# Stick-breaking heads: one summed softplus tile per key block in place of up to three products

## The chip, the cores and the metric

One NeuronCore of a Trainium2 chip runs the whole kernel as one program. The metric is the device time of one execution in microseconds (us). The engines are named as in the profile: PE is the matrix engine and PEld its weight loads, DVE the vector engine, ACT the scalar engine, POOL the general engine; SP issues most of the DMAs. Each engine works through its own list of instructions in order, and an instruction that waits holds back all that stand behind it on that engine.

## What is computed

One transformer block on 512 tokens of width 1024: 16 heads of stick-breaking attention, 4 heads of retention, two sigmoid branch gates, a gated merge and a feed-forward part, all in float32. The change touches the stick-breaking heads alone. Cut to what matters, per head:

```python
z = einsum('td,sd->ts', q, k) * scale           # queries t, keys s, in blocks of 128
mask = s_pos < t_pos
log_1m_beta = where(mask, log_sigmoid(-z), 0)   # = -softplus(z) where the mask holds
after = cumsum(log_1m_beta, reverse=True) - log_1m_beta   # sum over the later keys
a = where(mask, exp(log_sigmoid(z) + after), 0)
out = a @ v
```

For a key in block j, `after` is the sum over the later keys of its own block and over all keys of the later blocks. The cumulative sum runs over the keys, which lie on the partitions here (keys by queries), so it is made by matmuls: a triangular matrix of -1 for a block's own keys, a full matrix of -1 for each later block.

## The kernel before

Every float32 operand is split in two float32r parts: ACT copies it rounded (`hi`, L207) and DVE subtracts that from the source (`lo`, L209). A product with an exact operand (the -1 matrices) takes two matmuls, one for each part; a product of two split operands takes three.

The stick-breaking heads run in four groups of four, `sb_head(h)` for h = 0 to 15. A head has four key blocks j = 0 to 3; block j meets the queries from 128 j on, so its scores are 512, 384, 256 and 256 columns wide. `GEO` gives each block its PSUM bank: block 0 in bank 0, block 1 in bank 1, blocks 2 and 3 side by side in bank 2. The three banks `z` come from a pool of three, so a head's scores take the banks that the head before it gives free. A head is, for bank 2, 1, 0 in turn:

1. PE: the scores, k by q (`z<-q,q`), two matmuls for a block.
2. DVE: the mask by a minimum (L607), minus the absolute value by setting the sign bit (L609). ACT: exp (L612), log(1+x) (L613). DVE: max(z, 0) plus that, the softplus (L614). ACT and DVE: its split into `hi` and `lo`.
3. PE: `negtri` by the own block and `negones` by each later block, added to the scores in the bank. PE is the only engine that reads the softplus tiles.
4. ACT: exp of the bank (L630); ACT and DVE: split of it; PE: the product with v into the bank `av`. ACT copies `av` out (L642), a DMA on SP's list moves half of it to other partitions (L644), DVE adds the halves (L645).

Between the heads stand other pieces that PE can do meanwhile: `sb_qk(p)`, the q and k of a later pair of heads (48 matmuls 512 wide), whose results a DMA copies into tiles of the pool `q`, and 16 branch gates, `gate(i)` (24 matmuls 512 wide each, read by DVE in L827, then three activations). Their weights arrive by DMA and are split by ACT and DVE, 1024 columns at a time (`whi`, `wlo`). After the last head come the products with `w_proj_sb`, which need all heads.

The pool `q` has 8 buffers; a pair of heads holds three of them. The order of all instructions on each engine in this part is chosen by a scheduler when the program is built, from priorities (the program's order) and its own estimate of when operands are ready; nothing is written out by hand.

Of the kernel before, what the change touches and what calls it, by code (L numbers as in the profile page):

```python
# [19 lines left out]
P = 128  # L20
# [90 lines left out]
GEO = ((0, 0, 0, 512), (1, 0, 128, 384), (2, 0, 256, 256), (2, 256, 256, 256))  # L111
# [4 lines left out]
def kernel(  # L116
# [9 lines left out]
    nc = tc.nc  # L126
# [22 lines left out]
    def pair(tag):  # L149
        return apool.tile([P, 2, S], F32R, tag=tag, bufs=BUFS[tag], name=nm(tag))  # L150
# [44 lines left out]
    negtri = cpool.tile([P, P], F32R, name="negtri")  # L195
# [32 lines left out]
    def mm(o, lhs, rhs, start, stop):  # L228
        return nc.tensor.matmul(o, lhs, rhs, start=start, stop=stop, skip_group_check=True).ins  # L229
# [208 lines left out]
    with tc.manual_schedule(engines={nc.vector.engine, nc.scalar.engine, nc.tensor.engine}):  # L438

        nc.scalar.preload_act_table_set("natural_log_exp_and_others")  # L440
        c = sm[:, SM_C : SM_C + KT]
# [152 lines left out]
    def sb_head(h):  # L594
        q, k, vt = sbq[h], sbk[h], sbv[h // 4]
        z = [psz(), psz(), psz()]
        for j in (3, 2, 1, 0):
            bank, c, t0, w = GEO[j]
            for i in range(2):
                head_pe[h] = mm(z[bank][:, c : c + w], k[:, j * P : (j + 1) * P], q[:, i, t0:S],  # L600
                                i == 0 and j != 2, i == 1)
        sp = {}
        for bank in (2, 1, 0):
            w = BANKW[bank]
            zb = z[bank][:, :w]
            m = S if bank == 2 else P
            nc.vector.tensor_tensor(zb[:, :m], zb[:, :m], maskc[:, :m], op=ALU.min)  # L607
            t = tmp()[:, :w]
            nc.vector.tensor_scalar(  # L609
                t.bitcast(I32), zb.bitcast(I32), -(2**31), None, op0=ALU.bitwise_or  # L610
            )
            nc.scalar.activation(t, t, AF.Exp)  # L612
            nc.scalar.activation(t, t, AF.Ln, bias=1.0)  # L613
            nc.vector.scalar_tensor_tensor(t, zb, 0.0, t, op0=ALU.max, op1=ALU.add)  # L614
            hl = pair("s")
            split(hl[:, 0, :w], hl[:, 1, :w], t)
            sp[bank] = hl
        avs = {}
        for bank in (2, 1, 0):
            for j in (3, 2) if bank == 2 else (bank,):  # L620
                _, c, t0, w = GEO[j]
                terms = [(negtri, j, t0)] + [(negones, jj, GEO[jj][2]) for jj in range(j + 1, 4)]
                for lhs, jj, tt in terms:
                    bj, cj, tj, wj = GEO[jj]
                    for i in range(2):
                        mm(z[bank][:, c + tt - t0 : c + w], lhs, sp[bj][:, i, cj : cj + wj],
                           False, False)
            w = BANKW[bank]
            t = tmp()[:, :w]
            nc.scalar.activation(t, z[bank][:, :w], AF.Exp)  # L630
            hl = pair("s")
            split(hl[:, 0, :w], hl[:, 1, :w], t)
            avs[bank] = hl
        o = psa()
        r, hf = (h % 4) // 2, h % 2
        for j in (3, 2, 1, 0):
            bank, c, t0, w = GEO[j]
            v = vt[j // 2][:, j % 2, r * 256 + hf * P : r * 256 + hf * P + P]
            for i in range(2):
                mm(o[:, t0:S], v, avs[bank][:, i, c : c + w], j == 3 and i == 0, j == 0 and i == 1)  # L640
        u, u2 = tmp(), tmp()
        nc.scalar.activation(u, o, AF.Copy)  # L642
        own, oth = (slice(0, HD), slice(HD, P)) if hf == 0 else (slice(HD, P), slice(0, HD))
        nc.sync.dma_start(u2[own], u[oth])  # L644
        nc.vector.tensor_add(o_sb[h // 2][own], u[own], u2[own])  # L645
# [1082 lines left out]
```

## Time and profile before

| | |
|---|---|
| time, median of 3 runs | 1173.23 us (1172.66 to 1174.77) |
| span of the profiled execution | 1173.1 us |
| PE busy | 1156.8 us (99%), 6476 matmuls |
| DVE busy | 873.2 us (74%), 1342 instructions |
| ACT busy | 611.9 us (52%), 928 instructions |
| first mask (L607) of head 0, of head 1, of head 15 | 492.61, 502.44, 710.93 us |
| last product with v of head 15 | 726.80 us |

The page gives the profiled execution by its span, from its first to its last instruction; that is 0.1 us from the median of the runs, so spans and times can be compared as they stand. The heads take the stretch from about 490 to 727 us. A matmul's busy time contains the tail of its pipeline: what one costs in a stream is the distance from one start to the next, not its duration.

### The profile page before, as it was taken

To read this page: it belongs to the slowest core of one execution; us is meant where nothing else is said; L and a number is where in the kernel's file an instruction comes from. 1 tells how busy PE (TensorE), PEld (TensorE's weight loads), DVE (VectorE), ACT (ScalarE), POOL (GpSimd) and SP (SyncE) were. 2 spreads that over 40 slices of the span, in tenths; PEclk is the share of its full clock that TensorE was granted. 3 is DMA by queue.
4 is the path that set the end of the run, shared out by engine and by line. 5 is a ranking of instruction groups with operands and counts; after the bars stand their busy time and mean duration, and the time that the engine had idled before them with its cause. 6 is when DMAs were issued, how large, how long until landed. Compare 5 with 4: busy or idle time off the path is not lost.

```text
span 1173.1 us, 16899 instructions
## 1 busy us (share of the span) xinstructions
PE 1156.8 (99%) x6476; PEld 1010.9 (86%) x6476; DVE 873.2 (74%) x1342; ACT 611.9 (52%) x928; POOL 50.1 (4%) x84
## 2 busy tenths in 40 slices
PE   8999999999999999999999999999999999999996
PEld 7898888888878888888888888879999999999996
DVE  7979966775764867478888688775998776777556
ACT  5444543343333444478778688354954444454433
POOL 0000000020002010000000000000100000000000
PEclk9999999999999999999999999999999999999999
DMA  9723536493566565846565545873545663565232
GB/s 358 256 68 113 185 103 208 154 260 115 161 201 176 181 159 185 232 123 180 153 173 133 153 126 179 283 235 103 113 136 179 184 161 116 148 186 152 86 89 72
DMA packets 64017, 192.88 MB, mean 164 GB/s; under 512 B 7744, under 2 KB 9920, under 8 KB 63936
## 3 DMA queue, kind: packets, MB, share of 16 engines
q1 hardware_dynamic: 56624, 172.92, 46.3%
q0 software_dynamic: 6768, 18.35, 8.8%
q8 instruction: 51, 0.84, 0.3%
q10 hardware_dynamic: 544, 0.52, 0.1%
q14 instruction: 30, 0.25, 0.1%
HBM read 146.15 MB, written 18.87 MB: 141 GB/s over the span
## 4 chain that ended last, share of the span: by engine, by line
PE 89%; DVE 4%; DMA 3%; ACT 2%; issue 1%; SPq 0%; DVEq 0%; ACTq 0%
PE ps L229 65%; PE z L229 21%; PE av L229 3%; DMA raw<-wp 2%; DMA araw<-wada 1%; DVE sraw L387 1%; ACT whi L207 1%; DVE wlo L209 1%; DMA o<-xT 0%; ACT s L207 0%; DVE wlo L418 0%; DVE t L425 0%; DVE araw L257 0%; DMA gspill<-g 0%; DVE t L476 0%
## 5 line engine op out<-in xcount | busy, mean ns | idle before, releaser
L229 PE MATMUL ps<-h,whi 128*128 128x512 f32 (+1 forms) x1410 | 416.9, 377 | 1.6 <-DVE h L209 0.8
L229 PEld LDWEIGHTS ps<-h,whi 128*128 128x128 f32 x1410 | 256.2, 188 | 47.7 <-ACT h L431 1.8
L229 PE MATMUL ps<-h,wlo 128*128 128x512 f32 (+1 forms) x705 | 262.1, 376 | 0.0
L207 ACT ACTIVATE whi<-raw 128x1024 fp32r<-128x1024 f32 (+1 forms) x122 | 127.4, 1044 | 192.3 <-PE ps L229 144.8
L209 DVE TENSOR_TENSOR wlo<-raw,whi 128x1024 fp32r<-128x1024 f32 (+1 forms) x122 | 146.6, 1204 | 61.9 <-ACT whi L207 60.8
L229 PEld LDWEIGHTS ps<-h,wlo 128*128 128x128 f32 x705 | 132.8, 188 | 23.2
L229 PE MATMUL ps<-s,whi 128*128 128x512 f32 x480 | 148.5, 390 | 0.7 <-DVE v L209 0.6
L229 PE MATMUL z<-q,whi 128*128 128x256 f32 x504 | 106.8, 283 | 0.0
L229 PEld LDWEIGHTS ps<-s,whi 128*128 128x128 f32 x480 | 89.2, 188 | 19.3 <-DVE v L209 1.0
L229 PE MATMUL ps<-s,wlo 128*128 128x512 f32 x240 | 93.4, 389 | 0.0
L207 ACT ACTIVATE s<-t 128x512 fp32r<-128x512 f32 (+1 forms) x134 | 74.4, 586 | 34.8 <-DVE t L789 21.4
L209 DVE TENSOR_TENSOR s<-t,s 128x512 fp32r<-128x512 f32 (+1 forms) x134 | 81.3, 637 | 9.6 <-ACT s L207 9.3
L229 PEld LDWEIGHTS z<-q,whi 128*128 128x128 f32 x504 | 84.9, 192 | 1.5
L1166 DVE SCALAR_TENSOR_TENSOR o<-ps,mod,o 128x512 f32<-128x512 f32 (+1 forms) x63 | 42.4, 680 | 32.6 <-PE ps L229 32.6
L229 PEld LDWEIGHTS ps<-s,wlo 128*128 128x128 f32 x240 | 45.1, 188 | 9.5
L877 ACT ACTIVATE whi<-s 128x1024 fp32r<-128x1024 f32 x33 | 34.9, 1056 | 33.6 <-PE ps L229 19.0
L229 PE MATMUL ps<-whi,h 128*128 128x512 f32 (+1 forms) x192 | 52.4, 354 | 0.0
L881 DVE TENSOR_TENSOR wlo<-s,whi 128x1024 fp32r<-128x1024 f32 x32 | 39.1, 1222 | 16.3 <-ACT whi L877 15.9
L229 PE MATMUL ps<-q,whi 128*128 128x256 f32 (+1 forms) x224 | 49.3, 313 | 0.0
L229 PE MATMUL z<-qp,whi 128*128 128x256 f32 x168 | 47.2, 283 | 0.0
L229 PE MATMUL z<-q,wlo 128*128 128x256 f32 x168 | 46.4, 283 | 0.0
L257 DVE SCALAR_TENSOR_TENSOR araw<-araw,cact 128x1024 f32<-128x1024 f32 x32 | 38.4, 1221 | 10.0 <-DMA araw<-wada 9.8
(311 smaller groups left out, 2063.1 us busy)
## 6 DMA issues: line engine op xcount, KB each, us to landing
raw<-wp SPq DMA_DIRECT2D x151, 512.0 KB, 4.0
araw<-wada SPq DMA_DIRECT2D x32, 512.0 KB, 4.5
araw<-wp SPq DMA_DIRECT2D x26, 512.0 KB, 4.6
sraw<-wada SPq DMA_DIRECT2D x16, 512.0 KB, 7.8
q<-qp SPq DMA_DIRECT2D x32, 256.0 KB, 3.7
s<-wp SPq DMA_DIRECT2D x12, 512.0 KB, 5.2
spill<-o POOLq DMA_DIRECT2D x24, 256.0 KB, 7.2
o<-xT SPq DMA_DIRECT2D x16, 256.0 KB, 3.7
```

Of the source, the lines that this page charges most:

```text
L207: nc.scalar.activation(dst_hi, src, AF.Copy, scale=scale)
L209: return (eng or nc.vector).tensor_sub(dst_lo, src, f(dst_hi))
L229: return nc.tensor.matmul(o, lhs, rhs, start=start, stop=stop, skip_group_check=True).ins
L257: nc.vector.scalar_tensor_tensor(raw, raw, 1.0, cact, op0=ALU.mult, op1=ALU.mult, accum_out=col)
L387: nc.vector.scalar_tensor_tensor(raw, raw, 1.0, cact, op0=ALU.mult, op1=ALU.mult, accum_out=col)
L877: nc.scalar.activation(hi, t, AF.Copy)
L881: nc.vector.tensor_sub(lo, t, f(hi))
L1166: return nc.vector.scalar_tensor_tensor(x1[d][:, hv], o[:, hv], mod[:, gcol + d : gcol + d + 1], x1[d][:, hv], op0=ALU.mult, op1=ALU.add,)
```

## The change

`sb_head` makes two sums of softplus tiles on DVE, splits each of them as the tiles themselves are split, and gives them to `negones` in place of the tiles that they sum:

- When bank 2 is done (blocks 2 and 3), `late` = block 2 + block 3, 256 columns: one add (L620 in the new numbering), one copy on ACT, one subtraction on DVE. Block 1 multiplies `late` once, where it multiplied blocks 2 and 3.
- When bank 1 is done, `later` = block 1 + `late`, 384 columns in all (the add L625 covers 256 of them): again one add, one copy, one subtraction. Block 0 multiplies `later` once, where it multiplied blocks 1, 2 and 3.

`late` and `later` take buffers of the pool `q`. A head has 6 matmuls of 256 columns less on PE (2 for block 1, 4 for block 0), 4 instructions more on DVE and 2 more on ACT. From L628 on, line numbers of the new kernel are 13 higher than before: L630 is L643, L642 is L655, L645 is L658, L827 is L840.

```diff
--- before.py
+++ after.py
@@ -615,16 +615,29 @@
             hl = pair("s")
             split(hl[:, 0, :w], hl[:, 1, :w], t)
             sp[bank] = hl
+            if bank == 2:
+                late = pair("q")
+                nc.vector.tensor_add(t[:, 0:256], t[:, 0:256], t[:, 256:512])
+                split(late[:, 0, 0:256], late[:, 1, 0:256], t[:, 0:256])
+                t2 = t
+            elif bank == 1:
+                later = pair("q")
+                nc.vector.tensor_add(t[:, 128:384], t[:, 128:384], t2[:, 0:256])
+                split(later[:, 0, 0:384], later[:, 1, 0:384], t)
         avs = {}
         for bank in (2, 1, 0):
             for j in (3, 2) if bank == 2 else (bank,):
                 _, c, t0, w = GEO[j]
-                terms = [(negtri, j, t0)] + [(negones, jj, GEO[jj][2]) for jj in range(j + 1, 4)]
-                for lhs, jj, tt in terms:
-                    bj, cj, tj, wj = GEO[jj]
+                terms = [(negtri, t0, sp[bank][:, :, c : c + w])]
+                if j == 2:
+                    terms.append((negones, 256, sp[2][:, :, 256:512]))
+                elif j == 1:
+                    terms.append((negones, 256, late[:, :, 0:256]))
+                elif j == 0:
+                    terms.append((negones, P, later[:, :, 0:384]))
+                for lhs, tt, x in terms:
                     for i in range(2):
-                        mm(z[bank][:, c + tt - t0 : c + w], lhs, sp[bj][:, i, cj : cj + wj],
-                           False, False)
+                        mm(z[bank][:, c + tt - t0 : c + w], lhs, x[:, i, :], False, False)
             w = BANKW[bank]
             t = tmp()[:, :w]
             nc.scalar.activation(t, z[bank][:, :w], AF.Exp)
```

The scheduler orders the whole program anew. Three places are shown, word for word, before and now. In the names the number is that of the buffer; `ps` is a bank of a gate or of `sb_qk`, `z` and `av` are the banks of a head.

PE where head 8 starts, in the program before: the scores of head 8 (`z_5439`, `z_5438`, after `z_5440` a few rows earlier) and the products with v of head 7 (`av_5183`), and what follows.

```order
L229 MATMUL z_5438<-q_5266,q_5265 128x512 x2
L229 MATMUL ps_5787<-h_256,whi_5791 128x512
L229 MATMUL ps_5787<-h_256,wlo_5792 128x512
L229 MATMUL av_5183<-s_5180,v_3838 128x512
L229 MATMUL ps_5787<-h_303,whi_5791 128x512 x2
L229 MATMUL ps_5787<-h_303,wlo_5792 128x512
L229 MATMUL av_5183<-s_5180,v_3838 128x512
L229 MATMUL ps_5787<-h_350,whi_5791 128x512 x2
L229 MATMUL ps_5787<-h_350,wlo_5792 128x512
L229 MATMUL ps_5787<-h_398,whi_5791 128x512 x2
L229 MATMUL ps_5787<-h_398,wlo_5792 128x512
L229 MATMUL ps_5787<-h_445,whi_5791 128x512 x2
```

Eight more such rows, 12 matmuls of `ps`, follow until `z_5440<-s_5455,negtri`. Now the same place in the new program: the end of head 7 (`av_5199`), the scores of head 8 (`z_5456`, `z_5455`, `z_5454`) and its first `negtri`.

```order
L229 MATMUL av_5199<-s_5178,v_3978 128x256 x3
L229 MATMUL av_5199<-s_5187,v_3838 128x384 x2
L229 MATMUL av_5199<-s_5196,v_3838 128x512 x2
L229 MATMUL z_5456<-q_5282,q_5281 128x256 x4
L229 MATMUL z_5455<-q_5282,q_5281 128x384 x2
L229 MATMUL z_5454<-q_5282,q_5281 128x512 x2
L229 MATMUL ps_5890<-h_217,whi_5893 128x512
L229 MATMUL z_5456<-s_5471,negtri 128x256
L229 MATMUL ps_5890<-h_217,whi_5893 128x512
L229 MATMUL z_5456<-s_5471,negtri 128x256 x3
L229 MATMUL z_5456<-s_5471,negones 128x256 x2
L229 MATMUL z_5455<-s_5484,negtri 128x384 x2
```

The scores of head 8 now stand behind all of head 7, and one matmul of a gate (`ps_5890`) stands between them and the first `negtri`, where 25 of `ps` stood before.

DVE at the same place, before: masks of head 8 (L607), sign bits (L609), the softplus of bank 2 (L614), then the sum of the halves of head 7 (L645).

```order
L607 TENSOR_TENSOR z_5439<-z_5439,table_4023 128x128
L607 TENSOR_TENSOR z_5438<-z_5438,table_4023 128x128
L609 TENSOR_SCALAR t_5450<-z_5440 128x512
L609 TENSOR_SCALAR t_5459<-z_5439 128x384
L609 TENSOR_SCALAR t_5468<-z_5438 128x512
L614 SCALAR_TENSOR_TENSOR t_5450<-z_5440,t_5450 128x512
L645 TENSOR_TENSOR o_5022<-t_5192,t_5193 64x512
L614 SCALAR_TENSOR_TENSOR t_5459<-z_5439,t_5459 128x384
```

And now:

```order
L607 TENSOR_TENSOR z_5456<-z_5456,table_4023 128x512
L607 TENSOR_TENSOR z_5455<-z_5455,table_4023 128x128
L609 TENSOR_SCALAR t_5466<-z_5456 128x512
L609 TENSOR_SCALAR t_5479<-z_5455 128x384
L658 TENSOR_TENSOR o_5034<-t_5208,t_5209 64x512
L607 TENSOR_TENSOR z_5454<-z_5454,table_4023 128x128
L609 TENSOR_SCALAR t_5492<-z_5454 128x512
L614 SCALAR_TENSOR_TENSOR t_5466<-z_5456,t_5466 128x512
```

The sum of the halves of head 7 (L658, it was L645), which waits for a DMA, has moved ahead of the third mask and of the softplus of bank 2 (L614) of head 8.

PE at the end of the heads, before: scores and end of head 14 (`av_6350`), the scores of head 15 (`z_6365`, `z_6364`), then the last two gates (`ps_6599`, `ps_6636`).

```order
L229 MATMUL z_6365<-q_6018,q_6012 128x384 x2
L229 MATMUL z_6364<-q_6018,q_6012 128x512 x2
L229 MATMUL av_6350<-s_6347,v_6097 128x512
L229 MATMUL ps_6599<-h_350,whi_6602 128x512
L229 MATMUL ps_6599<-h_350,wlo_6603 128x512
L229 MATMUL av_6350<-s_6347,v_6097 128x512
L229 MATMUL ps_6599<-h_398,whi_6602 128x512 x2
L229 MATMUL ps_6599<-h_398,wlo_6603 128x512
L229 MATMUL ps_6599<-h_445,whi_6602 128x512 x2
L229 MATMUL ps_6599<-h_445,wlo_6603 128x512
L229 MATMUL ps_6599<-h_493,whi_6602 128x512 x2
```

Thirteen more rows of these two gates follow until the first `negtri` of head 15. Now, from the scores of head 15 (`z_6396`, `z_6395`, `z_6394`) to its products with the sums (`q_6414`):

```order
L229 MATMUL z_6396<-q_6042,q_6036 128x256 x4
L229 MATMUL z_6395<-q_6042,q_6036 128x384 x2
L229 MATMUL av_6380<-s_6359,v_6122 128x256
L229 MATMUL z_6305<-s_6348,negtri 128x512
L229 MATMUL z_6305<-q_6338,negones 128x384 x2
L229 MATMUL av_6380<-s_6359,v_6122 128x256 x3
L229 MATMUL av_6380<-s_6368,v_6121 128x384 x2
L229 MATMUL z_6394<-q_6042,q_6036 128x512 x2
L229 MATMUL av_6380<-s_6377,v_6121 128x512 x2
L229 MATMUL z_6396<-s_6411,negtri 128x256
L229 MATMUL z_6395<-s_6424,negtri 128x384
L229 MATMUL z_6396<-s_6411,negtri 128x256 x3
```

The last gate (`ps_6668`) now stands whole ahead of the first `negtri` of head 14, which is eight rows before this piece; no matmul of a gate is left between there and the first product with `w_proj_sb`.

DVE just ahead of that, in the new program: the softplus of head 14 (L614), the reading of the last gate's bank (L840), the low halves of head 14 and its sums (L620, L625).

```order
L614 SCALAR_TENSOR_TENSOR t_6317<-z_6307,t_6317 128x512
L614 SCALAR_TENSOR_TENSOR t_6330<-z_6306,t_6330 128x384
L840 TENSOR_SCALAR g_6699<-ps_6668,sm 128x512
L209 TENSOR_TENSOR s_6322<-t_6317,s_6322 128x512
L209 TENSOR_TENSOR s_6335<-t_6330,s_6335 128x384
L620 TENSOR_TENSOR t_6317<-t_6317 128x256
L614 SCALAR_TENSOR_TENSOR t_6343<-z_6305,t_6343 128x512
L625 TENSOR_TENSOR t_6330<-t_6330,t_6317 128x256
L209 TENSOR_TENSOR q_6325<-t_6317,q_6325 128x256
L209 TENSOR_TENSOR wlo_6833<-raw_6830,whi_6832 128x1024
```

The reading of the last gate's bank stands ahead of the low halves of head 14, which PE needs next.

## The prediction

> **What bounds the kernel now.** I read the page first, then the busy times cut at the start of each head, then the matmuls and waits inside a head.
>
> ```profile
> PE 1156.8 (99%) x6476; PEld 1010.9 (86%) x6476; DVE 873.2 (74%) x1342; ACT 611.9 (52%) x928; POOL 50.1 (4%) x84
> PE 89%; DVE 4%; DMA 3%; ACT 2%; issue 1%; SPq 0%; DVEq 0%; ACTq 0%
> ```
>
> PE is busy 99% of the span and carries 89% of the chain that ended last. The next view has one row for each head, from its first mask to that of the next; shown are heads 0, 4 and 14 and the sum over heads 0 to 14.
>
> ```profile
> 492.61:502.44 9.83, 9.83 (x52) 8.38 (x51) 9.12 (x16) 8.80 (x17) 0.00 (x0) 1.00 0.64 189
> ...
> 549.01:558.25 9.24, 9.24 (x49) 7.73 (x48) 9.18 (x17) 8.49 (x16) 0.00 (x0) 1.00 0.65 204
> ...
> 697.60:712.00 14.40, 14.40 (x75) 12.11 (x74) 12.81 (x22) 12.60 (x23) 0.00 (x0) 1.00 0.52 153
> sum 219.39, PE 219.34 PEld 183.54 DVE 179.78 ACT 173.68 POOL 0.00; mean PE 14.62 PEld 12.24 DVE 11.99 ACT 11.58 POOL 0.00
> ```
>
> After the length come PE, PEld, DVE and ACT. PE has no gap in any head. DVE has 39.6 us to spare over 15 heads, but nothing in head 4 (9.18 of 9.24): a head in which PE has little else to do takes as long as its vector work. PE stays full because gates and `sb_qk` stand between the steps of a head.
>
> **What is taken from PE.** One row groups the products with `negones` 256 wide; the pieces of the timeline give the price of one in a stream.
>
> ```profile
> L229 PE MATMUL z<-s,negones 128*128 128x256 f32 x160 | 26.8, 281 | 0.0
> ...
> 550.80 0.61 PE L229 MATMUL ps<-h,whi 128*128 128x512 f32 x2
> 551.25 0.39 PE L229 MATMUL ps<-h,wlo 128*128 128x512 f32 x1
> 551.48 0.61 PE L229 MATMUL ps<-h,whi 128*128 128x512 f32 x2
> ...
> 555.91 0.34 PE L229 MATMUL z<-s,negtri 128*128 128x384 f32 x1
> 556.09 0.65 PE L229 MATMUL z<-s,negones 128*128 128x256 f32 x4
> 556.57 0.63 PE L229 MATMUL ps<-h,whi 128*128 128x512 f32 x2
> ```
>
> From 556.09 to 556.57 four take 0.48 us: 0.12 each. Three 512 wide take 0.68 (550.80 to 551.48): 0.227 each; one 384 wide takes 0.18. Of the 160 products 96 go (6 in each of 16 heads): 96 x 0.12 = **11.5 us less for PE**, all of it on the path as long as PE stays full.
>
> **What is put on DVE and ACT.** No add or split 256 wide of these tiles is in the trace; the nearest are these.
>
> ```profile
> L900 DVE TENSOR_TENSOR s<-s,h 128x256 f32<-128x256 f32 x24 | 8.6, 419 | 0.0
> L209 DVE TENSOR_TENSOR s<-t,s 128x384 fp32r<-128x384 f32 x32 | 17.6, 551 | 0.5 <-ACT s L207 0.5
> L209 DVE TENSOR_TENSOR s<-t,s 128x512 fp32r<-128x512 f32 x64 | 43.3, 685 | 6.6 <-ACT s L207 6.3
> L207 ACT ACTIVATE s<-t 128x384 fp32r<-128x384 f32 x32 | 16.5, 515 | 0.4 <-DVE t L614 0.4
> 720.42 1.76 DVE L209 TENSOR_TENSOR s<-t,s 128x512 fp32r<-128x512 f32 x3
> ```
>
> Three in a row (512, 384, 512) take 1.76 where their durations add to 1.92: in a queue each costs about 0.08 less. So a head gets two adds at 0.35, a low half at 0.35 and one at 0.47, 1.5 us on DVE, and on ACT 0.4 (an estimate below the 0.515) and 0.5. Over 15 heads DVE goes from 179.8 to about 203 us of 219: on average it still fits. But in the heads with little cover it was full already, so I walk through the new order where the cover goes. In both walks time 0 is a point at which PE arrives without waiting, 512 wide vector work costs 0.6 in a queue, 0.68 alone, and these rows give the rest:
>
> ```profile
> 549.01 0.89 DVE L607 TENSOR_TENSOR z<-z,table 128x512 f32<-128x512 f32 x2
> 553.99 0.39 PE L229 MATMUL z<-s,negtri 128*128 128x256 f32 x1
> ...
> 520.87 0.60 ACT L642 ACTIVATE t<-av 128x512 f32<-128x512 f32 x1 [1.32 <-PE av L229]
> 524.03 0.69 DVE L645 TENSOR_TENSOR o<-t,t 64x512 f32<-64x512 f32 x1 [0.32 <-DMA t<-t]
> ...
> DVE g L827 <- PE ps L229: 14.0, 8, 3.3
> L827 DVE TENSOR_SCALAR g<-ps,sm 128x512 f32<-128x512 f32 x15 | 11.2, 747 | 14.0 <-PE ps L229 14.0
> L209 DVE TENSOR_TENSOR wlo<-raw,whi 128x1024 fp32r<-128x1024 f32 x28 | 34.1, 1220 | 7.2 <-ACT whi L207 7.0
> L207 ACT ACTIVATE whi<-raw 128x1024 fp32r<-128x1024 f32 x29 | 30.6, 1056 | 17.9 <-PE ps L229 17.7
> ```
>
> The shortest way from a head's first mask to its first `negtri` is head 4's, 4.98 us (549.01 to 553.99). From the end of the copy of `av` (521.47) the half that a DMA moves lies there 2.5 us later. DVE waited 14.0 us in all for gates' banks.
>
> *Heads 7 and 8.* Time 0 is the first `negtri` of head 7. DVE then has a weight's low half (to 2.0), the low halves of the two sums (2.8) and those of the three exp tiles, each behind its ACT copy (6.05). PE ends head 7 at 6.35 and has head 8's scores, which now stand behind it, by 7.65. The copy of `av` ends at 7.1, its DMA at 9.6; the sum of the halves (L658) waits for that ahead of the third mask, so the softplus of bank 2 ends at 11.65 (0.62, 0.22, 0.6, 0.65 after 9.6). ACT's copy then lets `negtri` start at 12.3; one matmul stood between. Copies and low halves of head 8 trickle in, with two tiles of `sb_qk` among them, and PE is through the next head's bank-2 scores at 15.6. In that stretch PE has 26 matmuls 256 wide, 10 of 384, 13 of 512: 7.9 us. **Lost: 7.7.**
>
> *Heads 14 and 15.* Time 0 is the end of the last gate. DVE reads its bank (L840) ahead of head 14's low halves: 0.9 and 1.5. Behind it ACT does the gate's first exp and a weight (2.4) before the copy of `late`; its low half is there at 3.6, then a weight's low half (4.75), that of `later` (5.2), block 0's (5.8), two exp tiles' (6.9), then head 15's masks (7.95). ACT copies the last exp tile at 8.15, DVE has its low half at 8.8, PE ends head 14 at 9.3. ACT's copy of `av` (9.9) stands ahead of head 15's exps, so its softplus of bank 2 ends at 12.1 and its first `negtri` is at 13.1. From there DVE has 14 instructions, which alternate with ACT's copies, to the last low half at 21.1; PE's last product ends at 21.4. PE has 28 matmuls of 256, 14 of 384, 20 of 512: 10.4 us. **Lost: 11.0.**
>
> *Head 4.* Between the last bank-2 score and `negtri` PE has 12 matmuls 512 wide of a gate and four scores, 3.5 us, where the way is at least 4.98. **Lost: 1.5.** In the other heads the matmuls that the new order puts there take 6 to 14 us and the way, with all that DVE has queued in it, 5 to 11; I count nothing for them.
>
> **The sum.** 1173.1 - 11.5 + 7.7 + 11.0 + 1.5 = **1181.8 us** (the span is 0.1 from the runs' median). The low end takes each loss by the trace of before: head 8's way 4.98 less 1.0 of cover, 4.0; head 15's way 4.98, then 6.4 to its last product,
>
> ```profile
> 710.93 0.69 DVE L607 TENSOR_TENSOR z<-z,table 128x512 f32<-128x512 f32 x1
> ...
> 720.61 0.28 PE L229 MATMUL z<-s,negtri 128*128 128x256 f32 x1
> ...
> 726.80 0.39 PE L229 MATMUL av<-s,v 128*128 128x512 f32 x1
> ```
>
> (720.61 to about 727.0), less PE's 8.3 in it (the 10.4 without the 2.1 ahead of head 15's bank-2 scores), 3.1; nothing at head 4: 1173.1 - 11.5 + 7.1 = 1168.7. The walks are nearer to the new order than these rows, so I take them.
>
> **Rivals.** *PE stays full.* If head 7's scores and the gates' order matter less than I read, the whole 11.5 us come out: 1161.6. For it speak the 99% and the 39.6 us that DVE has to spare; against it that head 4 has no slack and that two heads lose their cover. The Trainium skill, Perfetto Trace Analysis, section "Identifying the Most-Contended Engine", says to optimise the engine with the highest occupancy first (for Tensor judged by LDWEIGHTS busy), which is PE here on the page, 99% and 86%; by that rule alone the time would be this one.
>
> *The losses are the low ones*, because DVE and ACT run ahead of PE more than I assume: 1168.7 up to about 1175. For it speaks that the ways of 4.98 and 6.4 us are real stretches of the trace; against it that in neither a gate's bank, a DMA or a sum stands ahead of the step that PE needs.
>
> *PE's clock falls in the new gaps.* The trace shows this once, at its end:
>
> ```profile
> 1163.42 0.59 PE L229 MATMUL z<-t,ones 128*128 128x256 f32 x2
> 1166.30:1167.30 1.00, 0.00 (x0) 0.00 (x0) 0.97 (x3) 0.00 (x0) 0.00 (x0) 0.98 0.00 0
> 1167.30:1168.30 1.00, 0.00 (x0) 0.00 (x0) 1.00 (x3) 0.00 (x0) 0.00 (x0) 0.50 0.24 81
> ```
>
> The last matmul ends at 1164.0 and the granted clock is 0.50 from 1167.3 on, 3.3 us later. My gaps are 4.4 us (head 8) and 3.8 us (head 15), so both could reach it. How long the half clock then lasts no row shows; if as long as it takes to fall, each costs half of 3.3: 1181.8 + 3.3 = 1185.1. The Trainium skill, TensorE: Matmul & The Clock Gate, Part 1, gives windows of about 3.4 us in both directions; by that page each gap that spans a window costs 1.7 us. The trace agrees with the way down.
>
> **How the numbers follow.** Three runs lie within 2.1 us, so 0.2% (2.3 us) is about what can be told from no change. Chances: my sum, with its walks a few us off either way (1176 to 1187), 0.57; PE full 0.08; low losses 0.20, of which 0.06 below 1170.8 and 0.14 within 2.3 us of before; the clock on top 0.15, up to 1190. Faster 0.14, same 0.14, slower 0.72. The range 1169 to 1190 leaves out PE full and some of both ends.
>
> **What would show it.** Right: PE gaps of about 4 us ahead of the first `negtri` of heads 8 and 15, waiting for ACT's copy; DVE idle at L658 of head 8 for a DMA; PE's busy time over heads 0 to 15 lower than the stretch by 15 us or more; the products with `negones` 96 fewer and no other part of the kernel changed. Wrong: no PE gap over 2 us in the heads, or gaps in every head, which would mean that DVE is short throughout rather than at three places.

## Result and the profile after

The changed kernel takes 1187.53 us (median of 4 runs, 1186.67 to 1188.54) against 1173.53 us (1172.66 to 1174.77) for the program before on the same chip: a ratio of 1.0113, 95% interval 1.0100 to 1.0126, or 14.0 us slower. The profiled execution took 1188.54 us, its span is 1186.8 us: a span is 1.7 us or a little more below the time of its own execution. So the span 1173.1 of the program before goes with its slowest execution (1174.77), and that it lies 0.1 from the median is chance.

The page of the changed kernel: busy times, and the slices of the span for PE and its granted clock.

```profile
PE 1157.4 (98%) x6380; PEld 1005.1 (85%) x6380; DVE 896.2 (76%) x1406; ACT 624.3 (53%) x960; POOL 50.1 (4%) x84
PE   8999999999999999999989997999999999999996
PEclk9999999999999999999989998999999999999998
```

PE has 96 matmuls less than before (6476) and is busy no shorter (1156.8 before): it was busy for 14.8 us while the clock was at half (10.07 from 613.30 to 626.96, 4.68 from 732.78 to 739.61), so about 7 us of it are the slower clock (an estimate: half); the rest I put down to the tails of matmuls before gaps. The slice row has two dents, at slices 21 and 25, and the clock row has the same two: heads 7 and 8, and heads 14 and 15. The busy times in stretches of 5 us show them in detail; of the stretches from 485 to 745 these are all in which PE missed more than 0.7 us (columns: length, PE, PEld, DVE, ACT, POOL with counts, granted clock, DMA share, GB/s).

```profile
555.00:560.00 5.00, 3.32 (x15) 2.40 (x14) 4.90 (x10) 3.78 (x8) 0.00 (x0) 1.00 0.94 234
...
610.00:615.00 5.00, 4.21 (x13) 2.26 (x12) 3.78 (x7) 3.91 (x9) 0.00 (x0) 0.83 0.56 128
615.00:620.00 5.00, 3.48 (x10) 2.32 (x9) 3.18 (x7) 2.01 (x4) 0.00 (x0) 0.50 0.40 84
620.00:625.00 5.00, 2.93 (x10) 2.65 (x11) 4.97 (x11) 3.94 (x9) 0.00 (x0) 0.50 1.02 308
...
720.00:725.00 5.00, 3.18 (x14) 1.71 (x12) 5.00 (x11) 5.00 (x11) 0.00 (x0) 1.00 0.59 197
725.00:730.00 5.00, 4.23 (x19) 2.69 (x19) 4.25 (x10) 3.45 (x7) 0.00 (x0) 1.00 0.53 166
730.00:735.00 5.00, 0.77 (x2) 0.29 (x1) 3.23 (x7) 4.07 (x9) 0.00 (x0) 0.78 0.45 131
```

555 to 560 is head 4, 610 to 625 the change from head 7 to head 8, 720 to 735 heads 14 and 15. Before, PE missed 0.05 us from 485 to 730. What PE waited for, by the view of waits over 490 to 745:

```profile
PE z L229 <- ACT s L207: 5.3, 3, 3.6
PE ps L229 <- DVE qp L210: 5.3, 2, 3.6
PE z L229 <- ACT q L207: 2.0, 3, 0.9
```

The first row holds head 15's first `negtri`, the third the products with the sums (tiles in `q`). The second is new: a matmul of a gate waits for its bank `ps`, which still holds a result of `sb_qk` that DVE's L210 has to read. The timeline at head 8 shows what stood ahead of that; SP's rows are DMAs, put in order of time here with the other engines' rows of the same stretch.

```profile
608.91 0.67 SPq L567 DMA_DIRECT2D q<-qp  x1
616.17 0.60 ACT L655 ACTIVATE t<-av 128x512 f32<-128x512 f32 x1 [1.61 <-PE av L229]
616.79 0.46 SPq L657 DMA_DIRECT2D t<-t  x1
617.03 0.94 DVE L607 TENSOR_TENSOR z<-z,table 128x512 f32<-128x512 f32 x2 [1.74 <-PE z L229]
617.31 0.59 SPq L568 DMA_DIRECT2D q<-qp  x1
618.59 1.04 ACT L612 ACTIVATE t<-t 128x512 f32<-128x512 f32 x2 [1.82 <-DVE t L609]
...
620.50 0.60 ACT L207 ACTIVATE qp<-ps 128x512 fp32r<-128x512 f32 x1
...
621.33 0.68 DVE L210 SCALAR_TENSOR_TENSOR qp<-ps,qp 128x512 fp32r<-128x512 f32 x1
621.51 0.62 ACT L207 ACTIVATE s<-t 128x512 fp32r<-128x512 f32 x1
622.07 0.79 PE L229 MATMUL ps<-h,whi 128*128 128x512 f32 x1 [3.59 <-DVE qp L210]
622.66 0.41 PE L229 MATMUL z<-s,negtri 128*128 128x256 f32 x1
```

The gate's matmul, with head 8's first `negtri` right behind it on PE's list, starts after 3.59 us of idle, when L210 has read its bank. Two things lead up to L210, and they come together within 0.1 us. One goes over SP: it stands from 609.6 to 616.8 at L657, the DMA of head 7's output, which waits for ACT's copy of `av`; three copies from `qp` to `q` stand behind it, the first of them lands 3.1 us after its issue, at 620.4, and then ACT and DVE may write the tile `qp` again. The other is the order on ACT and DVE: both had waited for head 8's scores (1.74 us at the masks), and from 618.59 and 617.03 on they worked without a gap at head 8's masks, exps and softplus, behind which the copy into `qp` and L210 stand. The trace of the change alone doesn't tell which of the two was needed; the run with the clock kept, below, does, and it speaks for the second. Nor does the gate's matmul hold `negtri` back by the whole 3.59 us: ACT's copy of head 8's own softplus (621.51) ended at 622.13, so without that matmul `negtri` could have started about half a microsecond earlier (an estimate).

At head 15 the wait is the predicted one:

```profile
730.22 0.60 ACT L655 ACTIVATE t<-av 128x512 f32<-128x512 f32 x1 [1.71 <-PE av L229]
730.72 1.03 ACT L612 ACTIVATE t<-t 128x512 f32<-128x512 f32 x2
...
733.77 0.58 PE L229 MATMUL z<-s,negtri 128*128 128x256 f32 x1 [3.58 <-ACT s L207]
...
742.96 0.40 PE L229 MATMUL av<-s,v 128*128 128x512 f32 x1
```

ACT copies `av` of head 14, then makes head 15's exps, and PE waits 3.58 us for ACT's copy of the softplus.

### The profile page after: what moved, and what is told of

Its sections match the earlier page's. It is cut to its first block, busy times and chain, and to the rows that moved or that the text cites. A ratio compares the mean times of both kernels' runs of the same rounds, so it can differ in the third digit from the quotient of the medians.

```text
span 1186.8 us, 16781 instructions
## 1 busy us (share of the span) xinstructions
PE 1157.4 (98%) x6380; PEld 1005.1 (85%) x6380; DVE 896.2 (76%) x1406; ACT 624.3 (53%) x960; POOL 50.1 (4%) x84
## 4 chain that ended last, share of the span: by engine, by line
PE 89%; DVE 4%; DMA 3%; ACT 2%; issue 1%; SPq 0%; DVEq 0%; ACTq 0%
PE ps L229 66%; PE z L229 20%; PE av L229 3%; DMA raw<-wp 2%; DVE sraw L387 1%; ACT whi L207 1%; DVE wlo L209 0%; DMA araw<-wada 0%; DVE wlo L418 0%; DVE t L425 0%; DVE araw L257 0%; ACT s L207 0%; DMA q<-qp 0%; DMA spill<-g 0%; DMA t<-t 0%
## 5 line engine op out<-in xcount | busy, mean ns | idle before, releaser
L207 ACT ACTIVATE s<-t 128x512 fp32r<-128x512 f32 (+1 forms) x134 | 75.7, 587 | 36.5 <-DVE t L802 21.4
L894 DVE TENSOR_TENSOR wlo<-s,whi 128x1024 fp32r<-128x1024 f32 x32 | 39.1, 1222 | 16.5 <-ACT whi L890 16.2
L229 PE MATMUL z<-q,q 128*128 128x256 f32 (+2 forms) x224 | 47.1, 337 | 0.4 <-ACT t L643 0.4
```

The costliest lines, as they stand in the source:

```text
L207: nc.scalar.activation(dst_hi, src, AF.Copy, scale=scale)
L894: nc.vector.tensor_sub(lo, t, f(hi))
```

## The experiments

The theory at the start was that the 11.5 us are real, and that three places give back more, since the new order leaves no matmuls of gates or `sb_qk` there. The rivals were that DVE and ACT are short in every head, and that PE's half clock is what was lost. "In front of its first `negtri`" below is counted in the program's order, with the 0.227, 0.175 and 0.12 us that a matmul takes in a stream.

**The products alone.** The sums are left out:

```diff
-                late = pair("q")
-                nc.vector.tensor_add(t[:, 0:256], t[:, 0:256], t[:, 256:512])
-                split(late[:, 0, 0:256], late[:, 1, 0:256], t[:, 0:256])
...
-                later = pair("q")
-                nc.vector.tensor_add(t[:, 128:384], t[:, 128:384], t2[:, 0:256])
-                split(later[:, 0, 0:384], later[:, 1, 0:384], t)
...
-                    terms.append((negones, 256, late[:, :, 0:256]))
+                    terms.append((negones, 256, sp[2][:, :, 0:256]))
-                    terms.append((negones, P, later[:, :, 0:384]))
+                    terms.append((negones, P, sp[1][:, :, 0:384]))
```

> Block 1 and block 0 have one product with negones each, as in the change, but no sums are made: block 1 multiplies block 3's half of the bank-2 tile alone and block 0 multiplies block 1's tile alone, so the later blocks are left out. 96 matmuls of 256 columns less, nothing more on DVE or ACT. Theory (the matmuls are worth their stream time, and the time is lost only where the sums take the cover from heads 4, 8 and 15): full PE through all heads, 1173.5 - 11.5 = about 1162. Rival (the matmuls taken out were themselves the cover of a DVE that is short in every head): 1168 or more, with PE gaps in many heads.

1165.5 us, ratio 0.9935 (0.9920 to 0.9950): 8.6 us faster. PE's busy time falls by 10.6 us (1156.8 to 1146.2), close to the 11.5; PE then waits 1.9 us in the heads, once 1.2 and twice less. So the matmuls are worth nearly what was put on them, as long as nothing is added elsewhere.

**The sums alone.** They are made, and nothing reads them:

```diff
-                    terms.append((negones, 256, late[:, :, 0:256]))
+                    terms += [(negones, 256, sp[2][:, :, 0:256]), (negones, 256, sp[2][:, :, 256:512])]
```

(and in the same way for block 0.)

> The two sums are made and split as in the change, into the pool q, but nothing reads them: all products with negones are those of the program before. This is the cost of the added vector and copy work by itself. Theory (places, not load): in this program's order head 8 again has only 1.0 us of matmuls between its bank-2 scores and its first negtri, while head 4 has 7.6 and head 15 has 8.2, so only head 8's place is lost: 1173.5 + 8 to 11 = 1181 to 1185. Rival (DVE is short in all heads): 1173.5 + 25.5 = 1199, the change's whole loss without its saving. Rival (the added work is hidden): 1173.5.

1188.71 us, ratio 1.0131 (1.0116 to 1.0147): 14.6 us slower with all of PE's work still there. 14.6 is above the 8 to 11 of the theory and far below the 25.5 of a load that costs in every head. The two longest rows of PE's waits:

```profile
PE ps L229 <- DVE qp L210: 5.9, 1, 5.9
PE z L229 <- ACT s L207: 3.3, 1, 3.3
```

The first is head 8's, the second head 15's, each a single wait: the theory had left out head 15 because 8.2 us of matmuls stood in front of it.

**One place undone at a time.** The products of before in two heads, 7 and 8 in one kernel and 14 and 15 in the other, and the change in the rest:

```diff
+    OLD = (7, 8)
...
+            if h in OLD:
+                pass
-            if bank == 2:
+            elif bank == 2:
...
+                elif j < 2 and h in OLD:
+                    terms += [(negones, GEO[n][2], sp[GEO[n][0]][:, :, GEO[n][1] : GEO[n][1] + GEO[n][3]]) for n in range(j + 1, 4)]
```

> The change in all heads but 7 and 8, which have the products of before. In this order head 8 has 8.9 us of matmuls in front of its first negtri, where the change leaves 1.0; head 15 still has only 2.1. Theory: the loss at heads 7 and 8 read from the changed kernel's trace (18.7 us from the first negtri of head 7 to the end of head 9's bank-2 scores, with 7.9 us of PE work in it: 10.8) goes, less 2 x 0.72 of saving: 1187.5 - 9.4 = about 1178, and the granted clock stays at 1.00 from 600 to 640. Rival (DVE load everywhere): an eighth of 25.5 less 1.4, about 1185.7.

> The change in all heads but 14 and 15. Head 15 has 9.1 us of matmuls in front of its first negtri, where the change leaves 2.7; head 8 still has 1.0. Theory: the loss at heads 14 and 15 read from the changed kernel's trace (23.1 us from the end of the last gate to the last product with v, with 10.4 of PE work: 12.7) goes, less 1.4: 1187.5 - 11.3 = about 1176; the half clock stays at head 8 and goes at head 15. Rival (DVE load everywhere): about 1185.7.

With heads 7 and 8 as before: 1180.7 us, 6.8 us faster than the change (ratio to before 1.0064, 1.0049 to 1.0079). Head 8's wait for L210 is gone and the clock stays at 1.00 there; of the 9.4 expected 6.8 came. The end of the heads got worse: from 705 to 745 PE missed 9.4 us, in the change 7.3. With heads 14 and 15 as before: 1187.99 us (1185.57 to 1190.5), no gain where 11.3 was expected. This is the miss of the study. PE had its 9.1 us of matmuls, reached head 15's first `negtri` without a wait, and stopped behind it. Rows of DVE and PE from its timeline (L616 is the softplus there):

```profile
731.19 0.69 DVE L616 SCALAR_TENSOR_TENSOR t<-z,t 128x512 f32<-128x512 f32 x1 [1.01 <-ACT t L615]
735.05 0.68 DVE L664 TENSOR_TENSOR o<-t,t 64x512 f32<-64x512 f32 x1 [3.17 <-DMA t<-t]
735.66 0.54 DVE L616 SCALAR_TENSOR_TENSOR t<-z,t 128x384 f32<-128x384 f32 x1
...
736.82 0.98 PE L229 MATMUL z<-s,negtri 128*128 128x384 f32 x4 [3.77 <-ACT s L207]
```

L664 is the sum of the halves of head 14 (L658 in the change). It waits for its DMA ahead of the softplus of head 15's block 1; SP issued it at 730.39 and the landing took 4.6 us, the longest of 16 (median 2.3). So cover in front of the first `negtri` is not enough: the steps behind it have waits of their own. That is not all of the missing gain. From 720 to 745 PE was busy 20.67 us, 3.0 more than in the change; from 745 to 780 it was busy 32.63 us of 35, 2.4 less than in the change, because it waited there for the low halves of weights. The two heads also have 1.4 us of products more. PE's waits from 485 to 790 have this row, which the change has not:

```profile
PE ps L229 <- DVE wlo L209: 2.2, 2, 1.4
```

Why the weights came later there stays open. The profiled execution, 1185.57 us, was the fastest of the four.

**The pool of the sums.** The sums in `s` instead of `q`, first in a buffer each (only the pool's name differs from the change), then both in one tile, where block 0 takes the first 128 columns from block 1's own tile. The second edit:

```diff
-                late = pair("q")
+                late = pair("s")
...
-                later = pair("q")
...
-                split(later[:, 0, 0:384], later[:, 1, 0:384], t)
+                split(late[:, 0, 256:512], late[:, 1, 256:512], t[:, 128:384])
...
-                    terms.append((negones, P, later[:, :, 0:384]))
+                    terms += [(negones, P, sp[1][:, :, 0:P]), (negones, 256, late[:, :, 256:512])]
```

> The change as it is, but the two sums take buffers of the pool s (8, of which a head's tiles take six in turn) in place of the pool q, so that the q and k tiles of later heads no longer share their buffers with sums. In this order head 8 has 16.5 us of matmuls in front of its first negtri (1.0 in the change) and head 4 has 12.8; heads 13, 14 and 15 have 5.5, 3.5 and 2.9. Theory (buffers: sums in q hold back the q and k copies, the copies hold the tiles qp, those the banks ps; and the cover that one head uses up is missing at the end): the losses at heads 4, 5 and 8 go, head 15's 12.7 stays, heads 13 and 14 lose about 1 and 3: 1162 + 16.7 = about 1179, with PE never waiting for L210. Rival (the vector work itself is too much): 1187.

> As the run before, but the two sums share one tile of s: columns 0 to 255 hold late, 256 to 511 the last 256 columns of later; block 0 multiplies the first 128 columns of block 1's own tile besides. Two matmuls of 128 columns more per head (at most 0.1 us each, less what the 384 wide ones get narrower: 1 to 2 us in all) and 128 columns less for ACT and DVE. One buffer less per head; in this order only head 15 has little cover, 1.4 us. Theory: 1162 + 1.5 + 12.7 to 14 for head 15 = about 1177, with one place of PE gaps. Rival (vector load): about 1187 with gaps in several heads.

In a buffer each: 1207.76 us, ratio 1.0288 (1.0274 to 1.0302), where 1179 was expected. In one tile: 1183.25 us, ratio 1.0077 (1.0062 to 1.0093), where 1177 was expected. As the theory said, PE no longer waits for L210 in either; but the order also has 16.5 us of matmuls in front of head 8's first `negtri` in the first run, so this does not show what had held L210. But what head 8 gets back is lost at the end, and more: in the first, PE's gaps begin at 700 and last to 765. Two lists of one line's instructions (count, durations in ns, first and last start) tell why: the last reading of a gate's bank (L840) against the last mask (L607), in the change and then in the run with a buffer each.

```profile
L840 DVE TENSOR_SCALAR g<-ps,sm x16: 736/746/751, 475.8 to 720.5; 128x512 f32<-128x512 f32 x16
L607 DVE TENSOR_TENSOR z<-z,table x48: 290/300/700, 492.8 to 728.7; 128x128 f32<-128x128 f32 x32, 128x512 f32<-128x512 f32 x16
```

```profile
L840 DVE TENSOR_SCALAR g<-ps,sm x16: 740/749/751, 475.9 to 693.8; 128x512 f32<-128x512 f32 x16
L607 DVE TENSOR_TENSOR z<-z,table x48: 289/300/700, 492.9 to 751.8; 128x128 f32<-128x128 f32 x32, 128x512 f32<-128x512 f32 x16
```

The gates are done 8.2 us ahead of head 15's last mask in the change, and 58.0 us ahead here. In the program before they ended 13.0 us behind it (727.0 and 714.0). A head with sums has a longer way, the order puts more of the gates' matmuls into it (12 to 16 us in front of most first `negtri` in this run, 5 to 12 before), and there are only 16 gates: the last heads pay.

**Fewer heads with sums.** One tile in `s`, heads 8 to 11 with the products of before:

> As the run before in 12 heads; heads 8 to 11 have the products of before. Every head then has at least 7.8 us of matmuls in front of its first negtri (6.0 in head 0, as in the program before), head 15 has 9.0. Theory (the sums pay where cover is left over, and the loss is only the missing cover): no place is lost; saving 12 x 0.72 less 12 x 0.1 for the narrow matmuls = 7.4: about 1166, granted clock 1.00 throughout. Rival (vector load in every head with sums): 12/16 of 25.5 lost against 7.4 saved: about 1191.

1176.15 us, ratio 1.0021 (1.0012 to 1.0031); 1166 was expected, 1191 by the load. No gap is longer than 1.1 us, but there are many short ones; the longest row of PE's waits behind that for weights is

```profile
PE z L229 <- ACT s L207: 1.7, 6, 0.5
```

six waits; those at 566.0 and 582.2 stand in front of a product with the second sum, for which DVE has to add twice and ACT has to copy once more.

**The output's DMA on another queue.**

```diff
-        nc.sync.dma_start(u2[own], u[oth])
+        nc.gpsimd.dma_start(u2[own], u[oth])
```

> The change, with one edit: the DMA that moves half of av's copy (L657) is issued by POOL in place of SP, so that it no longer stands among the q and k copies on SP's list. In the changed kernel's trace SP stood from 609.6 to 616.8 at that DMA of head 7 with three q and k copies behind it; they landed at 620.4, let DVE's L210 read the ps bank at 621.3 and PE's gate matmul start at 622.07 after 3.59 idle. Theory (SP's list is a link of that chain): the wait for L210 at head 8 goes and the loss there falls from 10.8 to about 5, what 2.6 us of cover leave; head 15's 12.7 stays (cover 2.9): about 1182. Rival (SP's list is no link; the buffers come free no earlier): 1187 with the same 3.6 us wait for L210.

1208.13 us, ratio 1.0287 (1.0273 to 1.0301), 20 us above the change. The run doesn't answer the question: issued by POOL this DMA landed after 3.4 us (median of 16; 2.3 on SP), and DVE waited for it at the sum of the halves:

```profile
DVE o L658 <- DMA t<-t: 26.3, 13, 5.9
```

It was 4.1 us in 7 waits over the same stretch in the change. PE's wait for L210 did not go either (8.0 us in 2). Whether SP's list had held head 8 back is not told by this run.

**One sum alone, in two pools.** Only `late` is made. The two kernels differ in its pool alone; the edit of the first, of which the second leaves out the pool:

```diff
-                late = pair("q")
+                late = pair("s")
...
-                later = pair("q")
-                nc.vector.tensor_add(t[:, 128:384], t[:, 128:384], t2[:, 0:256])
-                split(later[:, 0, 0:384], later[:, 1, 0:384], t)
...
-                    terms.append((negones, P, later[:, :, 0:384]))
+                    terms += [(negones, P, sp[1][:, :, 0:384]), (negones, 256, late[:, :, 0:256])]
```

> Only the first sum is made (late, 256 columns, in a buffer of s); block 0 multiplies block 1's own tile and late. 64 matmuls of 256 columns less than before (64 x 0.12 = 7.7 us), and per head 2 instructions more on DVE and 1 on ACT (0.8 and 0.4 us) where the change has 4 and 2. late is made with bank 2, long before block 0 needs it. In this order every head but head 0 (6.0, as before) has 8.4 us or more of matmuls in front of its first negtri. Theory (the loss is missing cover, and the short waits of the run with one tile are for later, which comes last): full PE, 1174 - 7.7 = about 1166. Rival (every instruction more on DVE and ACT costs in each head): half of the change's 25.5 lost against 7.7 saved: about 1179.

> The same instructions as in the run with late alone in s, but late takes a buffer of q, as in the change. In this order head 8 has 1.0 us of matmuls in front of its first negtri, head 4 has 6.3, head 15 has 5.6. Theory (the pool q is what takes the cover from head 8): 1166 plus about 11 at head 8 and 1 at head 15 = about 1178, with PE waiting for L210 at head 8. Rival (the pool makes no difference): the same time as the run in s.

In `s` 1177.63 us, ratio 1.0032 (1.0020 to 1.0043); in `q` 1178.55 us, ratio 1.0036 (1.0023 to 1.0050). In `q` PE waits at head 8,

```profile
618.38 0.80 PE L229 MATMUL ps<-h,whi 128*128 128x512 f32 x1 [4.87 <-DVE qp L210]
```

and in `s` nowhere for L210: the pool does make that wait, by way of the order (1.0 us of matmuls in front of head 8's first `negtri` in `q`, 8.4 or more in `s`). The times differ by less than their intervals. In `s` the gates end 7.0 us ahead of head 15's last mask, in `q` 3.8 us behind it, and in `s` PE loses there part of what it saved at head 8 (from 605 to 625 it misses 5.2 us in `q`, none in `s`; from 705 to 765 3.4 in `q`, 5.9 in `s`). Rows of `s`:

```profile
725.10 0.68 DVE L653 TENSOR_TENSOR o<-t,t 64x512 f32<-64x512 f32 x1 [1.02 <-DMA t<-t]
...
726.90 0.63 PE L229 MATMUL z<-s,negtri 128*128 128x256 f32 x3 [1.63 <-DVE s L209]
729.17 1.54 PE L229 MATMUL z<-s,negtri 128*128 128x384 f32 x3 [1.40 <-DVE s L209]
```

**Sums in nine heads.** One tile in `q`; heads 7, 8 and 11 to 15 have the products of before:

```diff
+    OLD = (7, 8, 11, 12, 13, 14, 15)
```

> The two sums share one tile of q, and only heads 0 to 6, 9 and 10 make them; heads 7, 8 and 11 to 15 have the products of before. In this order every head has 7.6 us or more of matmuls in front of its first negtri (6.0 in head 0, as before), and heads 11 to 15, the last that can use the gates, ask for no more of them than in the program before. Saving 9 x 0.72 less 9 x 0.1 for the narrow matmuls = 5.6. Theory (a sum pays where the order still has matmuls to put in front, and the place where they run out is the end of the heads): 1168 to 1170, faster than before, with no PE gap over 1 us in the heads. Rival (each head with sums pays for its vector work): 9/16 of 25.5 lost against 5.6 saved: about 1182.

1170.41 us (1169.31 to 1170.7), ratio 0.9968 (0.9956 to 0.9981): faster than both kernels. All of PE's waits from 485 to 790 are two rows:

```profile
PE z L229 <- ACT s L207: 1.8, 1, 1.8
PE ps L229 <- DVE wlo L209: 0.5, 1, 0.5
```

One gap of 1.8 us remains (said: none over 1), and the time lies 0.4 above the 1168 to 1170 that was said. The gates end 3.4 us behind the last mask of head 15.

**The clock kept.** The change, with matmuls that only keep PE busy, in its gaps:

```diff
+    FILL = {8: 14, 15: 12}
+    STIR = {7: 5}
...
+        if h in FILL:
+            idle = psa()
+            for _ in range(FILL[h]):
+                mm(idle, negones, zcol.to_broadcast([P, S]), True, True)
...
+                    if j == 0 and lhs is negones and h in STIR:
+                        for _ in range(STIR[h]):
+                            mm(z[0], negones, zcol.to_broadcast([P, S]), False, False)
```

> The change, with matmuls added that only keep PE busy in its gaps: five that add zeros to block 0's bank of head 7, 14 into the free bank av at the start of head 8, 12 at the start of head 15. Seven of the 14 stand ahead of the scores of head 8 and wait for the copy of av. Theory (the half clock came with the gaps and did not make them: at head 8 the copies on SP's list hold the qp tile and the ps bank, at head 15 the copies and low halves on ACT and DVE set the pace): the granted clock is 1.00 through most of 613 to 627 and 733 to 739, and the time stays within 2 us of the change's, 1186 to 1189. Rival (the clock took what the prediction's walks missed): with the clock kept, half of the PE work in the 13.7 and 6.6 us at half clock comes back, about 6: 1181.5, near the predicted 1181.8.

1188.62 us, ratio 1.0124 (1.0109 to 1.0140): as the change, not 1181.5. At head 15 the clock stayed at 1.00, and its last product with v came at the same time as in the change, to the hundredth. The stretch from 727 to 744 of the change, of this run, and this run's last product:

```profile
727.00:744.00 17.00, 11.48 (x46) 8.68 (x45) 13.54 (x27) 13.62 (x28) 0.00 (x0) 0.80 0.31 101
```

```profile
727.00:744.00 17.00, 13.92 (x60) 10.07 (x59) 15.52 (x29) 15.49 (x31) 0.00 (x0) 1.00 0.54 168
...
742.96 0.40 PE L231 MATMUL av<-s,v 128*128 128x512 f32 x1
```

From head 15's first `negtri` to that product it is 9.19 us in the change (from 733.77) and 8.64 here (from 734.32). So at head 15 the half clock cost about half a microsecond at most: ACT and DVE set the pace. At head 8 the run doesn't separate the clock from the rest. The half clock lasted 6.8 us in all there in place of 13.7, but seven of the added matmuls wait for the copy of `av` and put the scores of head 8 off (615.93 to 617.77), and from head 7's first `negtri` to head 8's it took 18.0 us (605.80 to 623.84) where the change takes 15.0. The equal time is thus made of unequal parts. What the clock cost the change at head 8 stays open, between nothing and 5.0 us (an estimate: half of the 10.07 us in which PE was busy there at half clock).

The same run answers the question about SP's list at head 8. L570 (L568 in the change) is issued there at 615.11, 2.2 us earlier than in the change, and lands 3.1 us later, at 618.2. Yet DVE reads the bank later, at 622.76 (L212; L210 at 621.33 in the change):

```profile
618.52 0.90 DVE L616 TENSOR_TENSOR z<-z,table 128x512 f32<-128x512 f32 x2 [5.14 <-PE z L231]
...
621.92 0.57 ACT L209 ACTIVATE qp<-ps 128x512 fp32r<-128x512 f32 x1
...
622.76 0.68 DVE L212 SCALAR_TENSOR_TENSOR qp<-ps,qp 128x512 fp32r<-128x512 f32 x1
```

The tile `qp` had been free for 3.7 us when ACT wrote it; DVE had no gap from head 8's first mask (618.52) to L212. So the reading of the bank follows head 8's own scores and masks, behind which it stands on ACT's and DVE's lists, and not SP's copies. The run with the sums alone agrees: there the copy of 616.49 landed at 620.2, and ACT's copy into `qp` started at 621.43.

**The runs together.** Time between the last reading of a gate's bank and head 15's last mask (positive: the gates still cover the last head), for the program before and the runs in which PE never waits for L210 at head 8:

| kernel | last gate less last mask, us | time, us |
|---|---|---|
| before | 727.0 - 714.0 = 13.0 | 1173.5 |
| products alone | 712.2 - 706.1 = 6.1 | 1165.5 |
| one tile, 9 heads | 719.7 - 716.3 = 3.4 | 1170.4 |
| one tile, 12 heads | 713.8 - 719.3 = -5.5 | 1176.2 |
| late alone in `s` | 713.6 - 720.6 = -7.0 | 1177.6 |
| heads 7, 8 as before | 709.7 - 722.8 = -13.1 | 1180.7 |
| one tile in `s` | 706.8 - 726.8 = -20.0 | 1183.3 |
| sums in `s` | 693.8 - 751.8 = -58.0 | 1207.8 |

In the six rows with sums the time rises as the gates end earlier, by 0.6 us for each microsecond on average (0.4 to 0.9 from row to row). Part of that is built into the column: head 15's last mask carries the time that was lost before it, and in every row the time is 454 to 460 us above that mask. The end of the last gate alone puts these six rows in the same order, but not the products alone, whose gates end at 712.2 with 2.9 of the 11.5 us lost: few gates cost only where the heads' way is longer too. The change itself (-8.2), the sums alone (3.5, with all of PE's work) and `late` alone in `q` (3.8) lie above the line of the six; all three have 1.0 us of matmuls in front of head 8's first `negtri` and the wait there. That the heads with sums run out of gates fits all rows; no run changed the number of gates alone, so it is not shown by itself.

## Why the prediction was right or wrong

It said slower with 0.72, at 1181.8 in a range of 1169 to 1190; it is slower, at 1187.5, inside the range and 5.7 above the number. The direction and the places came from the mechanism; that the range held owes something to luck, for the sum's own band ended at 1187, and only the part for the clock reached further. The sum also starts from the span 1173.1, 0.4 below the median of 1173.53. By its steps:

- *The 11.5 us of PE.* Near: 10.6 us of busy time in the run with the products alone, 8.6 us of time.
- *Three places, not all heads.* Right. PE misses 14.3 us from 485 to 745, where "15 us or more" was said, nearly all at heads 4, 7 to 8 and 14 to 15; the runs with heads 7 and 8 undone and with sums in 9 and 12 heads came out 5 to 15 us below what a loss in every head with sums would have made.
- *Heads 14 and 15, 11.0.* Right in cause, low by 1.7. Counted from the end of the last gate (720.09), head 15's masks began at 7.0 us (6.9 in the walk), its first `negtri` at 13.7 (13.1), its last product at 22.9, ending at about 23.1 (21.4). With PE's 10.4 us that is 12.7 lost. Its gap of 3.58 us waits for ACT's copy, as written.
- *Heads 7 and 8, 7.7.* The step that failed: 10.8 lost. Counted from head 7's first `negtri` (607.70), head 7 ended at 8.2 (6.35 in the walk): its last low half was done at 7.6 (6.05), since DVE waited 0.53 and 0.59 us for ACT's copies. Head 8's eight scores ran at half clock, 2.35 us where their prices in a stream add to 1.3, and were through at 10.6 (7.65). The wait of L658 for its DMA, which the walk put ahead of head 8's softplus, did not come: L658 ran at 619.07 without any idle time. The softplus of bank 2 ended at 13.7 (11.65), ACT's copy of it at 14.4 (12.3). So the late end of head 7 and the slow scores, not the DMA, set the softplus back by 2.1 us. The last half microsecond to `negtri` at 15.0 is the gate's matmul ahead of it, which the walk counted as cover and not as a waiter: its bank was read by L210, behind that softplus on DVE's list. The next head's bank-2 scores were through at 18.7 (15.6).
- *Head 4, 1.5.* 1.7 us measured (the 5.3 of the wait for L210 less head 8's 3.59). The trace names L210, but ACT's copy of head 4's softplus ended at 559.72, just after the gate's matmul had started (559.68): the softplus was as late as the walk said. Head 5 lost 0.9 more, unforeseen, in front of a product with a sum.
- *The sum.* -11.5 + 10.8 + 12.7 + 1.7 + 0.9 = +14.6, against 14.0 measured.
- *PE stays full*, 1161.6. Fell. The rule of the Trainium skill, Perfetto Trace Analysis, "Identifying the Most-Contended Engine", held only where nothing was put on other engines: the products alone gave 1165.5.
- *The clock on top*, 1185.1 to 1190. The measured time lies there and the clock did fall at both places, so the result alone would have spoken for this rival. The run with the clock kept speaks against it at head 15 (half a microsecond at most) and leaves it open at head 8, where 2.35 us for the scores is part of the loss above. What the number lacked was 3.1 us at heads 7 and 8, some of them perhaps the clock's, and 1.7 at heads 14 and 15.
- *The DMA wait at the sum of the halves.* Right mechanism, wrong place: 3.17 us at head 15 with heads 14 and 15 undone, 26.3 us on POOL's queue.

## What to carry to other kernels

When an engine is full because other work is put between the steps of a chain, that work is a stock: making the chain longer on other engines uses it up earlier, and the bill comes where it runs out, so look at when the last piece of it ends. Before giving a temporary a buffer of a shared pool, look at what it does to the order of the whole program: `late` in `q` instead of `s` left head 8 with 1.0 us of matmuls in front of its first `negtri`. A matmul that stands in front of a step as cover can be a waiter itself, so see what holds its bank. When a trace names one chain behind a wait, look for a second that ends at the same time, and for a run in which the two come apart. Apply such a change only where cover is left over: sums in 9 of 16 heads gained 3.7 us where sums in all lost 14.0.

## What the runs showed of the hardware

The granted clock changes on a fixed raster. In the change it is half from 613.30 to 626.96 and from 732.78 to 739.61, in the run with the clock kept from 614.50 to 617.92 and from 624.74 to 628.16: 4, 2, 1 and 1 times 3.41 us, with 31 times 3.41 between the two of the change. Cut along that raster, the change and then the run with the clock kept read so:

```profile
609.89:613.30 3.41, 2.62 (x10) 1.37 (x9) 2.93 (x5) 2.79 (x7) 0.00 (x0) 1.00 0.85 196
613.30:616.71 3.41, 3.41 (x11) 2.27 (x10) 1.25 (x2) 1.77 (x4) 0.00 (x0) 0.50 0.00 0
...
623.54:626.96 3.42, 3.42 (x14) 3.05 (x14) 3.06 (x7) 2.36 (x6) 0.00 (x0) 0.50 1.03 261
722.54:725.95 3.41, 2.37 (x13) 1.47 (x11) 3.41 (x7) 3.41 (x8) 0.00 (x0) 1.00 0.52 154
```

```profile
611.09:614.50 3.41, 2.36 (x7) 1.14 (x7) 1.25 (x2) 2.06 (x4) 0.00 (x0) 1.00 0.01 2
614.50:617.92 3.42, 3.29 (x8) 2.66 (x9) 0.00 (x0) 0.07 (x1) 0.00 (x0) 0.50 0.64 132
```

Unexpected is that no idle window is needed. The clock fell after windows with 10 and 7 matmuls in them, with PE shown busy 2.62 and 2.36 us of 3.41 (tails included) and weight loads 1.37 and 1.14 us; it held after one with 13 and 1.47 us. It came back only after a window with weight loads of 2.66 us or more, not after one with 2.27. The Trainium skill, TensorE: Matmul & The Clock Gate, Part 1, states a free-running window of 3413 ns: by that page the raster is expected, and these edges agree with it. It speaks of an idle window for the way down, which these rows do not bear out.
